# Zero products at the head and in four gaps of TensorE's program, token copies on VectorE, shared PSUM places for the leading tiles

## The chip, the core and the metric

The kernel runs on one core of one Trainium2 chip. The metric is the device time of one launch in microseconds (us), the median over several runs. PE is TensorE's matmul stream, PEld its weight loads, DVE is VectorE, ACT ScalarE, POOL GpSimdE and SP SyncE, which here only issues transfers.

## The reference

Two layers of a diffusion trunk run over 512 latent tokens and 128 context tokens of width 2048, all in float32. Cut to what matters here:

```python
for layer in range(DEPTH):                      # 2 layers: even, odd
    sh_p, sc_p, gt_p = modulation(c_ctx, ada_w[layer], ada_b[layer])   # silu(cond) @ w + b, three parts
    sh_s, sc_s, gt_s = modulation(c, ada_w[layer], ada_b[layer])
    hp = rms_norm(xp, norm_g[layer]) * (1.0 + sc_p) + sh_p
    hs = rms_norm(xs, norm_g[layer]) * (1.0 + sc_s) + sh_s
    # input projection h @ w_in, two mixers (attention / short conv or two attentions),
    # SiLU gates, output projection
    xp = xp + gt_p * out_p
    xs = xs + gt_s * out_s
```

So before the first large product (layer 0's h @ w_in) can start, the kernel needs the tokens with their features on the partitions, each token's norm factor, and the scale and shift parts of the modulation, which are themselves products of silu(cond) with 2048-row weights.

## The kernel before, in words

All products take a float32 weight and a float32 operand apart into a high and a low part and add three products (`proj_q`, `one_block`, `lead_units`). The split of a weight is an ACT copy (line 227) and a DVE subtraction (line 228).

The order on each engine is not the order of the source: a planner at build time puts the instructions of each engine into a fixed order, by their place in the source, by what they wait for and by its own times. `tc.issue_after(x)` pins what the block emits on the engine of `x` behind `x`. At run time each engine goes through its own order and waits where something isn't ready.

**The head.** `x_load` brings five blocks of 128 tokens, two halves each, on ACT's and SP's queues. The conditions `c` and `c_ctx` land in rows 0 to 31 of `rows_a`; a Tanh on ACT (`th`, line 122) and a DVE step (line 123) make SiLU of them, PE transposes them (line 126) and DVE writes `sT`, the operand of every modulation product. `first_loads` then gives the order of the head: `x_block` for each block of tokens, `vec_rows` (transposes of small vectors, line 131), `ada_on_pe` for the scale of the first 128 features, `x_rows` (the norm factors spread over all partitions, lines 975 and 976), and `ada_on_pe` for the shift.

`x_block` transposes a block in four groups of four 128x128 transposes (line 960), each group into a PSUM place of `psT` (two places, tag T, shared by every small use in the kernel), and copies each group to `xT` (line 961): groups 0 to 2 on DVE, group 3 on ACT. ACT squares each half of a block into a PSUM place (line 965) for the norm, DVE and POOL finish it (lines 967 to 969).

`ada_on_pe` loads 1 MB or more of modulation weights (line 169, four buffers), multiplies on PE (line 180, 32 instructions for 16 products: a full-precision product is two instructions), copies, transposes (line 186) and reduces.

**The leading tiles.** `lead_units` then runs eight column tiles of the input projection at once, two rows of features (k) at a time, while the modulation for the next features is still being made: `make_h(k)` is `h0_maker`, `ahead` is `ada_group`, the modulation of the features to come. Unit 0 takes k = 0 (`c = 0`) and k = 1 (`c = 1`) one after the other. Six of the tiles are summed in SBUF and pass through PSUM place 0 (`new_pp(0)`, halves pa and pb), two (`held`) stay in PSUM. The first products are on lines 359 to 361, those of later units on lines 263 to 265. Weight pieces of these tiles come through buffers of tag `raw` (four of them), which `rows_a`, `rows_b` and `th` also use before.

After that `run_tiles` goes on tile by tile. `new_pp` gives PSUM places in turn and writes each into the list `whole`; `bank_of` gives a job that has staged such a tile the tile's own PSUM place for its transposes, and otherwise a T place. Of the leading tiles this concerns the key tile (`k_gen`: staged by `stage`, line 626, transposed on line 633, read on lines 663 to 668).

## Time and profile before

| what | value |
|---|---|
| three runs | 2281.19, 2277.36, 2281.74 us (median 2281.19) |
| the profiled execution's own time | 2278.45 us |
| its span, first to last instruction | 2276.6 us |
| DVE, ACT, POOL busy | 1602.2, 1087.0, 162.7 us |
| granted clock | 1.0 in every window of the profile |
| moved | 337.64 MB, mean 148 GB/s |

A row of the timeline gives start and length in us, engine, line, operation, output and inputs, shape, count, and in brackets the engine's idle time before it and what ended it. A row of the groups gives count, busy us and mean ns, then idle us before and its causes. Ends of matmuls are modelled, and they are pipelined, so starts are to be read rather than ends.

### The profile page before, as it was taken

The page shows a single profiled execution, that of the slowest core. Times are in us where ns is not written, and L with a number is a line of the kernel's source. Part 1 is how long each engine was busy: PE and PEld are TensorE (multiplying, and loading weights), DVE is VectorE, ACT ScalarE, POOL GpSimd, SP SyncE. Part 2 cuts the span into 40 slices and gives each one's busy share as a digit, 9 for nine tenths or more (in the row PEclk, how much of TensorE's full clock was granted, in tenths as well). Part 3 has the DMA queues.
Part 4 walks back from the last instruction along what each step waited for, and adds up shares of the span by engine and source line. Part 5 has one row for each costly group of instructions (what it writes and reads, how often), then busy time and mean ns, then how long its engine had stood idle before and what let it go on. Part 6 is the DMA issues. An engine that isn't in the chain of part 4 may idle for free.

```text
span 2276.6 us, 41019 instructions
## 1 busy us (share of the span) xinstructions
PE 2245.3 (99%) x15941; PEld 2173.6 (95%) x15941; DVE 1602.2 (70%) x2830; ACT 1087.0 (48%) x2281; POOL 162.7 (7%) x226
## 2 busy tenths in 40 slices
PE   7999999999999999999999999999999999999999
PEld 5889999999999999999999999999999999999999
DVE  5666969779779777887797666565666655557865
ACT  5224535245352222544474444565565676754443
POOL 1001000010000000000100001111111100000101
PEclk9999999999999999999999999999999999999999
DMA  9975545655647565745553333423223221238542
GB/s 323 321 224 174 178 148 165 184 162 169 182 122 231 174 189 158 231 146 148 163 167 105 115 111 113 146 70 100 86 61 101 69 64 57 71 105 256 150 134 62
DMA packets 382514, 337.64 MB, mean 148 GB/s; under 512 B 16098, under 2 KB 342208, under 8 KB 381808
## 3 DMA queue, kind: packets, MB, share of 16 engines
q1 hardware_dynamic: 367744, 290.10, 42.7%
q0 software_dynamic: 13856, 42.76, 5.5%
q8 instruction: 125, 2.05, 0.4%
q10 hardware_dynamic: 720, 2.16, 0.3%
q14 instruction: 69, 0.57, 0.1%
HBM read 295.37 MB, written 39.59 MB: 147 GB/s over the span
## 4 chain that ended last, share of the span: by engine, by line
PE 90%; DMA 4%; DVE 2%; ACT 2%; issue 2%; SPq 0%; POOL 0%; POOLq 0%; ACTq 0%; DVEq 0%
PE pq L606 7%; PE pq L605 7%; PE pq L604 7%; PE pa L263 6%; PE pa L264 6%; PE pb L264 6%; PE pb L263 6%; PE pb L265 6%; PE pa L265 6%; PE pa L277 3%; PE pb L278 3%; PE pb L279 3%; PE pb L277 3%; PE pa L279 3%; PE pa L278 3%; PE T L808 2%
## 5 line engine op out<-in xcount | busy, mean ns | idle before, releaser
L227 ACT ACTIVATE wh<-raw 128x512 fp32r<-128x512 f32 x418 | 263.7, 631 | 545.0 <-PE pb L264 384.9
L228 DVE TENSOR_TENSOR wl<-raw,wh 128x512 fp32r<-128x512 f32 x418 | 288.0, 690 | 199.9 <-ACT wh L227 191.9
L263 PE MATMUL pa<-h,wh 128*128 128x320 f32 x978 | 310.1, 318 | 3.4 <-ACT h L227 1.7
L264 PE MATMUL pa<-h,wh 128*128 128x320 f32 x978 | 304.3, 312 | 2.0 <-DVE h L228 1.8
L265 PE MATMUL pa<-h,wl 128*128 128x320 f32 x978 | 302.9, 310 | 0.0
L264 PE MATMUL pb<-h,wh 128*128 128x320 f32 x978 | 302.5, 309 | 0.0
L265 PE MATMUL pb<-h,wl 128*128 128x320 f32 x978 | 302.4, 309 | 0.0
L263 PE MATMUL pb<-h,wh 128*128 128x320 f32 x978 | 301.6, 309 | 0.7 <-ACT h L1435 0.7
L205 DVE SCALAR_TENSOR_TENSOR acc<-adaw,sT,acc 128x1024 f32<-128x1024 f32 x240 | 300.6, 1280 | 0.2 <-DMA adaw<-in_ada_w 0.2
L604 PE MATMUL pq<-h,wh 128*128 128x320 f32 x672 | 208.6, 310 | 0.0
L606 PE MATMUL pq<-h,wl 128*128 128x320 f32 x672 | 207.7, 309 | 0.0
L605 PE MATMUL pq<-h,wh 128*128 128x320 f32 x672 | 207.7, 309 | 0.0
L263 PEld LDWEIGHTS pa<-h,wh 128*128 128x128 f32 x978 | 183.6, 188 | 16.6 <-issue 9.1
L264 PEld LDWEIGHTS pa<-h,wh 128*128 128x128 f32 x978 | 184.0, 188 | 7.8 <-issue 4.1
L263 PEld LDWEIGHTS pb<-h,wh 128*128 128x128 f32 x978 | 183.3, 188 | 1.4 <-ACT h L1435 0.9
L264 PEld LDWEIGHTS pb<-h,wh 128*128 128x128 f32 x978 | 183.6, 188 | 0.9 <-issue 0.8
L265 PEld LDWEIGHTS pa<-h,wl 128*128 128x128 f32 x978 | 183.7, 188 | 0.4 <-issue 0.4
L265 PEld LDWEIGHTS pb<-h,wl 128*128 128x128 f32 x978 | 183.6, 188 | 0.0
L605 PE MATMUL pq<-T,wh 128*128 128x320 f32 x504 | 155.2, 308 | 0.0
L606 PE MATMUL pq<-T,wl 128*128 128x320 f32 x504 | 155.1, 308 | 0.0
L604 PE MATMUL pq<-T,wh 128*128 128x320 f32 x504 | 155.0, 308 | 0.0
L277 PE MATMUL pa<-h,wh 128*128 128x320 f32 x448 | 146.5, 327 | 0.0
(488 smaller groups left out, 5410.8 us busy)
## 6 DMA issues: line engine op xcount, KB each, us to landing
adaw<-in_ada_w SPq DMA_DIRECT2D x128, 512.0 KB, 4.2
raw<-in_ev_w_in SPq DMA_DIRECT2D x176, 256.0 KB, 3.4
raw<-in_od_w_in SPq DMA_DIRECT2D x154, 256.0 KB, 2.9
ada<-in_ada_w SPq DMA_DIRECT2D x32, 1024.0 KB, 9.7
w<-in_od_w_in SPq DMA_DIRECT2D x27, 512.0 KB, 3.9
yd<-y POOLq DMA_DIRECT2D x32, 320.0 KB, 3.3
w<-in_ev_w_out SPq DMA_DIRECT2D x18, 512.0 KB, 4.7
w<-in_od_w_out SPq DMA_DIRECT2D x18, 512.0 KB, 4.3
```

Of the source, the lines that this page charges most:

```text
L205: V.scalar_tensor_tensor(out=acc[c], in0=w, scalar=sT[:, kt, c:c + 1], in1=acc[c], op0=ALU.mult, op1=ALU.add)
L227: A.activation(hi, x, AF.Copy)
L228: V.tensor_sub(lo, x, hi)
L263: PE.matmul(ps, wh[:, i, :], hi[:, sl], start=(j == js[0] if alone else (pos == 0 and j == 0)), stop=False)
L264: PE.matmul(ps, wh[:, i, :], lo[:, sl], start=False, stop=False)
L265: last_mm[j % 4] = PE.matmul(ps, wl[:, i, :], hi[:, sl], start=False, stop=(j == js[1] - 1 if alone else (pos == 3 and j == 3)))
L277: PE.matmul(ps, wh[:, j, :], hi[:, sl], start=(qd == 0 and j == 0), stop=False)
L278: PE.matmul(ps, wh[:, j, :], lo[:, sl], start=False, stop=False)
L279: PE.matmul(ps, wl[:, j, :], hi[:, sl], start=False, stop=(qd == 3 and j == 3))
L604: PE.matmul(ps, wh[:, j, :], hi, start=(new and h == 0 and j == 0), stop=False, **kw)
L605: PE.matmul(ps, wh[:, j, :], lo, start=False, stop=False, **kw)
L606: PE.matmul(ps, wl[:, j, :], hi, start=False, stop=(h == 1 and j == 3), **kw)
```

## The change

1. A tile `cold` of zeros is made on DVE; ACT takes a Tanh of one column of it ahead of all else.
2. `keep_warm(n)` multiplies `cold` with itself n times on PE into a PSUM tile that nobody reads: 14 times ahead of the first transpose, 8 times after block 0 and its vectors, 4 times within block 1, 6 times between the two calls of `x_rows`, 4 times behind the shift product.
3. `x_block` transposes into PSUM places pa0, pb0, pa1, pb1 of the projection in place of the two T places; all copies but one (block 3, group 3) go to DVE; the squares are written to SBUF (tag h5) in place of PSUM.
4. The scale product stands between blocks 3 and 4 in the source, before it stood behind block 4.
5. The modulation of feature block 1 (`ahead(0, (1, 2))`) stands at leading tile 3 in place of tile 1, its PE instructions pinned behind the last product so far.
6. `rows_a`, `rows_b` and `th` get tiles of their own in place of weight buffers.
7. Five small loads (gains, band, sink) are pinned behind the last modulation load on SP.
8. `new_pp` writes only the later tiles into `whole`, so the jobs of leading tiles transpose into T places.
9. The first weight splits of the leading tiles are pinned on ACT behind the last square of block 4 in place of its last copy.

```diff
+    cold = pre.tile([P, P], F32, name="cold")
+    V.memset(cold, 0.0)
+    A.activation(cold[:, 0:1], cold[:, 0:1], AF.Tanh)
+    rows_a = pre.tile([P, P], F32, name="rows_a")
...
+    warm = pS.tile([P, 1024], F32, tag="S", name="warm")
+    def keep_warm(n):
+        for _ in range(n):
+            PE.matmul(warm[:, 0:P], cold, cold, start=True, stop=True)
+    keep_warm(14)
...
-    def new_pp(i):
+    def new_pp(i, own=False):
...
-        whole.extend(pp)
+        if own:
+            whole.extend(pp)
...
-                    if i == 1 and ui == 0 and c == 0:
-                        ahead(0, (1, 2))
-                    elif i == 1 and ui + 1 < len(units):
+                    if i == 3 and ui == 0 and c == 0:
+                        with tc.issue_after(last_mm[0].ins):
+                            ahead(0, (1, 2))
+                    elif i == 1 and (ui or c) and ui + 1 < len(units):
                         ahead(*units[ui + 1][1:])
...
-            pp = new_pp((i - lead) % 2)
+            pp = new_pp((i - lead) % 2, True)
...
+    sqj = hpool.tile([P, 1024], F32, tag="h5", name="sqj")
     def x_block(b, ts):
-            ta = psT()
+            ta = pproj.tile([P, 512], F32, tag="p" + ("a0", "b0", "a1", "b1")[g], name="ta")
...
-            put[0] = (A.copy if g == 3 else V.tensor_copy)(xT[g][:, :, b * P:(b + 1) * P],
+            (A.copy if g == 3 and b == 3 else V.tensor_copy)(xT[g][:, :, b * P:(b + 1) * P],
...
+            if b == 1 and g == 1:
+                keep_warm(4)
             if g % 2 == 0:
-                junk = pS.tile([P, 1024], F32, tag="S", name="sqj")
-                A.activation(junk, ts[g // 2], AF.Square, accum_out=s4[:, g // 2:g // 2 + 1])
+                put[0] = A.activation(sqj, ts[g // 2], AF.Square, accum_out=s4[:, g // 2:g // 2 + 1])
...
         x_block(0, xs[0])
         vec_rows(0, 80, rows_a, 32)
-        for b in range(1, 5):
+        keep_warm(8)
+        for b in range(1, 4):
             x_block(b, xs[b])
+        ada_on_pe(0, 4, 0, 1, scale)
+        x_block(4, xs[4])
         last_act[0] = put[0]
-        ada_on_pe(0, 4, 0, 1, scale)
         x_rows((0, 1, 2, 3))
+        keep_warm(6)
         x_rows((4,))
         vec_rows(80, 77, rows_b, 0)
         ada_on_pe(0, 0, 0, 1, shift)
+        keep_warm(4)
```

More of the change, by code (lines that the diff above doesn't have):

```diff
@@ L94, in trunk_kernel @@
     sp = pre = pools["cur"]
-    rows_a = wpool.tile([P, P], F32, tag="raw", name="rows_a")
+    cold = pre.tile([P, P], F32, name="cold")
+    V.memset(cold, 0.0)
+    A.activation(cold[:, 0:1], cold[:, 0:1], AF.Tanh)
+    rows_a = pre.tile([P, P], F32, name="rows_a")
     def x_load(b):
@@ L109, in trunk_kernel @@
     xs = [x_load(b) for b in range(5)]
-    rows_b = wpool.tile([P, P], F32, tag="raw", name="rows_b")
+    rows_b = pre.tile([P, P], F32, name="rows_b")
     nc.gpsimd.dma_start(rows_b[0:48, :], I["ada_b"][1].rearrange("(k p) -> k p", p=P))
@@ L115, in trunk_kernel @@
         nc.gpsimd.dma_start(rows_b[74 + i:75 + i, :], I[n])
+    last_ada = [None]
     ada_t = [pre.tile([P, 2048], F32, name=f"ada{i}") for i in range(4)]
@@ L119, in trunk_kernel @@
     h_t = [pre.tile([P, NT], F32, name=f"ht{i}") for i in range(2)]
-    th = wpool.tile([32, P], F32, tag="raw", name="th")
+    warm = pS.tile([P, 1024], F32, tag="S", name="warm")
[3 more added lines that the diff above has]
+    keep_warm(14)
+    th = pre.tile([32, P], F32, name="th")
     A.activation(th, rows_a[0:32, :], AF.Tanh, scale=0.5)
@@ L168, in ada_load @@
         ada_t.append(ada_t.pop(0))
-        nc.sync.dma_start(w, I["ada_w"][l, kt * P:(kt + m) * P, cb * 512 + b0 * P:cb * 512 + (b0 + n) * P]
+        last_ada[0] = nc.sync.dma_start(w, I["ada_w"][l, kt * P:(kt + m) * P, cb * 512 + b0 * P:cb * 512 + (b0 + n) * P]
                           .rearrange("(k p) n -> p k n", p=P))
@@ L960, in x_block @@
                 PE.transpose(ta[:, j * P:(j + 1) * P], ts[g // 2][:, o:o + P], ident)
-            put[0] = (A.copy if g == 3 else V.tensor_copy)(xT[g][:, :, b * P:(b + 1) * P],
-                                                           ta.rearrange("p (j t) -> p j t", j=4))
+            (A.copy if g == 3 and b == 3 else V.tensor_copy)(xT[g][:, :, b * P:(b + 1) * P],
+                                                             ta.rearrange("p (j t) -> p j t", j=4))
+            if b == 1 and g == 1:
+                keep_warm(4)
             if g % 2 == 0:
-                junk = pS.tile([P, 1024], F32, tag="S", name="sqj")
-                A.activation(junk, ts[g // 2], AF.Square, accum_out=s4[:, g // 2:g // 2 + 1])
+                put[0] = A.activation(sqj, ts[g // 2], AF.Square, accum_out=s4[:, g // 2:g // 2 + 1])
         ss = small.tile([P, 1], F32, tag="nm", name="ssx")
@@ L981, in ada_group @@
         if g == 3 and js[1] == 4:
-            for i, n in enumerate(("a_k_norm", "c_k_norm", "d_k_norm")):
-                load_rows(gain_rows[:, i, :], n)
-            nc.sync.dma_start(band, I["k_band"])
-            load_rows(sink, "a_sink")
+            with tc.issue_after(last_ada[0].ins):
+                for i, n in enumerate(("a_k_norm", "c_k_norm", "d_k_norm")):
+                    load_rows(gain_rows[:, i, :], n)
+                nc.sync.dma_start(band, I["k_band"])
+                load_rows(sink, "a_sink")
     def first_loads(cols):
```

## The prediction

> **What bounds the kernel now.** I read the page first, then the table by windows, then the timeline of the first 36 us, then the waits and the neighbourhood of the first key tile.
>
> ```profile
> span 2276.6 us, 41019 instructions
> PE 2245.3 (99%) x15941; PEld 2173.6 (95%) x15941; DVE 1602.2 (70%) x2830; ACT 1087.0 (48%) x2281; POOL 162.7 (7%) x226
> ```
>
> TensorE (PE) is busy for 99% of the span. So a change in the head is worth what it takes off the moment from which PE no longer stops; nothing behind that moment shortens by it.
>
> ```profile
> 0.00:10.00 10.00, 1.34 (x6) 1.28 (x7) 1.06 (x5) 3.27 (x5) 4.37 (x12) 1.00 0.80 267
> 20.00:30.00 10.00, 7.76 (x104) 5.58 (x102) 6.35 (x15) 4.73 (x11) 0.55 (x1) 1.00 1.15 315
> 30.00:40.00 10.00, 8.24 (x101) 6.78 (x102) 6.00 (x16) 6.18 (x15) 0.00 (x0) 1.00 1.12 336
> 40.00:50.00 10.00, 10.00 (x99) 6.45 (x98) 3.36 (x9) 3.57 (x9) 0.00 (x0) 1.00 1.00 307
> 150.00:160.00 10.00, 10.00 (x105) 7.66 (x105) 5.89 (x16) 1.38 (x3) 0.00 (x0) 1.00 0.43 116
> ```
>
> Columns: the window, its length, busy us (and count) of PE, PEld, DVE, ACT, POOL, then granted clock, DMA share, GB/s. PE idles for 8.7, 2.2 and 1.8 us in the first three rows and not in the fourth. The transfers are full (share 1.00 to 1.15, 307 to 336 GB/s) from 20 to 50 us and half idle (0.43) by 150 us: in the head, loads are a second bound right behind PE.
>
> ```profile
> 6.68 1.28 ACT L122 ACT_TABLE_LOAD   x1 [6.68 <-DMA rows_a<-in_c_ctx]
> 8.65 0.31 PE L126 MATMUL T<-ident,rows_a 32*128 32x32 f32 x1 [8.65 <-DVE rows_a L123]
> 8.89 3.87 PE L960 MATMUL T<-ident,xb 128*128 128x128 f32 x16
> 12.36 1.03 ACT L965 ACTIVATE sqj<-xb 128x1024 f32<-128x1024 f32 x1 [0.67 <-DMA xb<-in_x_sample]
> 19.11 1.14 PE L960 MATMUL T<-ident,xb 128*128 128x128 f32 x8 [0.19 <-DVE xT L961]
> 21.99 1.14 PE L960 MATMUL T<-ident,xb 128*128 128x128 f32 x8 [0.19 <-DVE xT L961]
> 24.77 0.59 ACT L961 COPY xT<-T 128x512 f32<-128x512 f32 x1 [2.35 <-PE T L960]
> ```
>
> PE's first work waits until 8.65 for a Tanh whose table load starts only when its rows have landed. The first 16 token transposes take 3.87 us (0.24 each); later 8 take 1.14 (0.14). Blocks of 16 then repeat every 2.88 us (19.11 to 21.99), with PE waiting for copies out of two PSUM places; the last copy ends at 25.36.
>
> ```profile
> 26.50 1.29 PE L975 MATMUL T<-ident,rx 128*128 128x128 f32 x10
> 28.45 1.08 PE L180 MATMUL T<-ada,sT 128*32 128x128 f32 x32
> 31.16 1.08 PE L180 MATMUL T<-ada,sT 128*32 128x128 f32 x32 [0.86 <-DMA ada<-in_ada_w]
> 32.18 0.56 PE L359 MATMUL pa<-h,wh 128*128 128x320 f32 x2
> 34.63 1.08 PE L180 MATMUL T<-ada,sT 128*32 128x128 f32 x32 [0.90 <-DMA ada<-in_ada_w]
> 35.64 0.42 PE L360 MATMUL pa<-h,wh 128*128 128x320 f32 x1
> ```
>
> The leading tiles start at 32.18; the shift product that they need starts at 28.45, 3.73 us earlier. Two modulation loads then hold PE for 0.86 and 0.90 us. From 35.64 on PE no longer stops for the head.
>
> **The change, part by part.** *Early table load.* A Tanh on a memset tile takes the load (1.28) off the wait for rows_a: the first transpose moves from 8.65 to about 7.4. On the other side, standing ahead of the input loads that ACT issues, it could hold them by the same 1.28, and the head with them; it waits for a memset while they wait for nothing, so I take the gain.
>
> *14 zero products at the head.* L975 shows the form: five full-precision products are ten instructions in 1.29 us, 0.26 per product. They run from about 2 us, when only loads are under way. At the slow rate of the first 16 transposes (0.24 per instruction) 28 instructions take 6.7 us, at the later one 3.9: they end between 6 and 8.7, against 7.4 for the first real transpose, so they cost between 0 and 1.3. I take 0.3. What they bring: block 0's transposes drop from 3.87 to some 2.2.
>
> *22 zero products in four gaps* (8, 4, 6, 4): 22 x 0.26 = 5.7 us of PE. Twelve stand among transposes, where PE needs 4 x 16 x 0.14 = 9.0 of the 4 x 2.88 = 11.5 us of four blocks and also waits for block 1 (the ACT row at 12.36 shows its second half landing at 12.3); that covers their 3.1 us. The six (1.6) and the last four (1.0) stand around the norm rows and the shift product, in the stops between 27.8 and 32.2. Without that cover they put up to 2.6 us on the chain. As clock keepers I price them at nothing: the transposes at 19.11 already run at the fast rate with nothing but transposes ahead of them. [...]
>
> *Copies.*
>
> ```profile
> L227 ACT ACTIVATE wh<-raw 128x512 fp32r<-128x512 f32 x418 | 263.7, 631 | 545.0 <-PE pb L264 384.9
> ...
> L965 ACT ACTIVATE sqj<-xb 128x1024 f32<-128x1024 f32 x10 | 10.3, 1027 | 0.8 <-DMA xb<-in_x_sample 0.7
> L961 DVE COPY xT<-T 128x512 f32<-128x512 f32 x15 | 10.1, 690 | 3.2 <-PE T L960 2.9
> L961 ACT COPY xT<-T 128x512 f32<-128x512 f32 x5 | 2.9, 582 | 2.4 <-PE T L960 2.3
> L967 DVE TENSOR_REDUCE ssx<-s 128x1 f32<-128x2 f32 x5 | 0.8, 153 | 0.3 <-ACT sqj L965 0.2
> ```
>
> Four of ACT's five copies go to DVE: 4 x 0.69 = 2.76 and two small operations of 0.15 make at most 3.06 us of DVE a block, somewhat less where copies overlap in part. That is the old pace of 2.88, not a faster one. The gain is that four PSUM places (pa, pb) replace two, so PE and ACT no longer wait in turn. With block 0 copied by 10.8, block 1 bound by its landing (12.3, done by 14.3) and three blocks at 2.9, the last copy ends at about 22.9 instead of 25.36. The squares now write SBUF; 1.03 us, or by two of the 512-wide writes to SBUF (631 ns) at most 1.3, twice a block, stays under DVE's 3.
>
> *Scale product ahead of the last block.*
>
> ```profile
> L169 SPq DMA_DIRECT2D ada<-in_ada_w x1: 520/520/520, 10.9 to 10.9; - x1
> DMA to landing us min/median/max: 10.2/10.2/10.2
> ...
> L169 SPq DMA_DIRECT2D ada<-in_ada_w x1: 467/467/467, 18.1 to 18.1; - x1
> DMA to landing us min/median/max: 7.2/7.2/7.2
> ...
> L169 SPq DMA_DIRECT2D ada<-in_ada_w x1: 2532/2532/2532, 35.8 to 35.8; - x1
> DMA to landing us min/median/max: 11.8/11.8/11.8
> 47.30 1.93 PE L180 MATMUL T<-ada,sT 128*32 128x256 f32 x32
> ```
>
> The scale load lands at 10.9 + 10.2 = 21.1, the shift load at 18.1 + 7.2 = 25.3. If PE meets the scale product ahead of block 4, block 4's transposes, copies, norm and rows queue behind a stop until 21.1: 1.08 + 4 x 0.69 + 0.6 brings the last copy to about 25.5, and no gain is left in that chain but its overlap. If block 4 goes first, the shift load is the bound: 25.3 + 3.73 = 29.0 for the leading tiles, against 32.18. I take 29.2, **3.0 us earlier**; the other order gives about 30.7, 1.5 earlier.
>
> *Modulation of block 1 behind lead tile 2.* It moves two loads' products behind three leading tiles (18 products) and so behind their landings (31.1 and 34.6); the 0.86 and 0.90 us of stops go, but 1.08 us of product that lay ahead of 32.18 now lies behind: even, 0.
>
> *rows_a, rows_b, th out of the weight buffers.*
>
> ```profile
> SPq L336 <- DVE mod L163: 4.0, 1, 4.0
> ```
>
> SP stood 4.0 us at a weight load until a buffer came free. That stop goes; since the transfers are full, little lands earlier (0 to 0.8 us). The five small loads pinned behind the last modulation load keep their place: 0.
>
> *Leading key tile frees its own PSUM.*
>
> ```profile
> 198.53 0.60 PE L633 MATMUL pa<-ident,stg 128*128 128x128 f32 x4
> 201.60 0.69 DVE L665 TENSOR_TENSOR kg<-pa,gain_rows 128x512 f32<-128x512 f32 x1
> 202.35 0.42 PE L263 MATMUL pa<-h,wh 128*128 128x320 f32 x1 [1.71 <-DVE kg L665]
> ```
>
> The key tile transposes into pa, and the next tile's products wait 1.71 us until kg has been read. With a shared T place pa is free as soon as it is staged: **1.7 us** go, at best. At worst PE meets the next transpose, which needs a T place too, with both held until 202.3, and the stop stays: 0.
>
> Sum on the profiled execution: 2278.45 (span 2276.6) - 3.0 - 1.7 = 2273.75. The median of the runs, 2281.19, lies 2.74 above that execution; the same 4.7 off gives 2276.5, or 0.21%.
>
> **Rivals.** *Capped by the loads.* PE's order is fixed beforehand. The fourth load of the next unit lands at 35.8 + 11.8 = 47.6; its second half of products in the block at 47.30 starts near 48. That leaves about 0.4 us. If the block keeps its place in the order while all moves up by 3.0, PE stops there for the rest and the head yields only 0.4 to 1.3. For it: the full share from 20 to 50 us. Against: behind 47.30 there are still unit-0 products that the order can draw ahead, and SP's 4.0 us stop goes. With the key tile: 1.5 to 3.0 off, 2278.2 to 2279.7.
>
> *The change doesn't do what it says.* The zero products wait for nothing, so the plan may put all 36 at the front: 72 instructions, 28 slow (6.7) and 44 at 0.13 (5.7), until about 14 us, past block 0's data. The head then ends where it did, with the key tile's 0 to 1.7: about 2280.5.
>
> *Slower: scores ahead of their softmax.*
>
> ```profile
> PE S L820 <- ACT p L794: 2.1, 4, 1.5
> ```
>
> The order behind the head is planned anew. Today score products wait for the softmax that still holds S four times, 1.5 us at the longest. If the new order puts the two attention stages a step earlier, each such place costs 1.5; the even layer has 40 score steps (4 pairs of heads, 5 blocks, 2 heads). It decides from four such stops, which eat the 4.7; at seven it is 10.5 - 4.7 = 5.8 slower, 2287. For it: a gap that closes early moves every filler. Against: only one long stop today, with the same plan rules.
>
> **How the numbers follow.** What a measurement of this kernel can tell from no change is about 0.2%, 4.6 us. The forecast case (head 2.5 to 4, key tile 1 to 1.7) has 0.46, capped 0.29, no effect 0.08, slower 0.17. Of the forecast case nearly all but 0.06 lies beyond 0.2%, and 0.02 of the capped one with luck elsewhere: faster 0.42; same 0.06 + 0.27 + 0.08 = 0.41; slower 0.17. The range: the forecast case with its upper bounds (head 4.1, that is the shift load's 3.2 and one of the two stops; key tile 1.7; two of the 1.5 us stops gone by luck) is 8.8 off, 2272; at the other end no effect and the mild slower outcomes, +3, 2284; beyond lies some 0.2.
>
> **What would show it.** Right: the first transpose near 7.4 and 16 of them in about 2.2 us; last xT copy near 23; L359 near 29; no DMA stop over 1 us at L180 from 38 to 50; no wait of L263 on kg. Capped: L180 waiting on ada for 1.5 to 3 us near 45. All products in front: L960 starting past 10. Slower: L820 waits above 8 us in total. I am wrong in kind if L359 starts later than 31.5, or if PE's waits behind 210 us change by more than the head does.

## The result, and the profile after

The changed kernel takes 2284.71 us (median of 7 runs, 2283.12 to 2287.5) against 2277.36 (7 runs, 2275.66 to 2281.95): ratio 1.0029, 95% interval 1.0019 to 1.0038. (The 2281.19 that I forecast from was the median of the first three of the seven runs before.) The change costs some 6.6 us (the interval says 4.3 to 8.7), where I had forecast 4.7 us less. The profiled execution, page first, then the table by windows (window, length, busy us of PE, PEld, DVE, ACT, POOL, then granted clock, DMA share, GB/s):

```profile
span 2283.2 us, 41163 instructions
...
PE 2258.0 (99%) x16013; PEld 2185.8 (96%) x16013; DVE 1602.1 (70%) x2835; ACT 1083.9 (47%) x2278; POOL 162.2 (7%) x226
```

```profile
0.00:10.00 10.00, 7.26 (x43) 7.26 (x44) 1.63 (x6) 3.54 (x6) 4.36 (x12) 1.00 0.77 254
20.00:30.00 10.00, 7.58 (x62) 6.39 (x63) 3.86 (x11) 4.21 (x9) 1.10 (x2) 0.66 1.05 298
30.00:40.00 10.00, 7.99 (x93) 6.77 (x96) 5.42 (x15) 4.63 (x11) 0.99 (x1) 1.00 1.13 323
40.00:50.00 10.00, 9.88 (x115) 6.83 (x107) 3.62 (x10) 5.05 (x14) 0.00 (x0) 1.00 0.92 283
```

The span is 6.6 us longer and PE is busy 12.7 us longer, with 72 instructions more (the 36 zero products). The new thing stands in the second row: from 20 to 30 us the granted clock is 0.66, and PE gets through 62 instructions where it did 104. (The 1.00 of the first row is no measurement up to 8.01 us: the first full clock is on record there, before at 12.65.) All seven runs of the changed kernel have a mean granted clock of 0.997 or 0.998, while 22 of the 27 runs of before measured beside b_ahead have 0.999 or 1.000, so the profiled execution is no exception. The timeline of PE in the head shows why:

```profile
2.74 5.89 PE L129 MATMUL warm<-cold 128*128 128x128 f32 x28 [2.74 <-ACT cold L97]
8.47 1.91 PE L975 MATMUL ta<-ident,xb 128*128 128x128 f32 x16
...
22.41 0.64 PE L192 MATMUL T<-ada,sT 128*32 128x128 f32 x2 [3.09 <-DMA ada<-in_ada_w]
22.98 1.97 PE L975 MATMUL ta<-ident,xb 128*128 128x128 f32 x8
24.88 1.93 PE L192 MATMUL T<-ada,sT 128*32 128x128 f32 x30
26.74 1.76 PE L975 MATMUL ta<-ident,xb 128*128 128x128 f32 x7
...
30.38 1.95 PE L129 MATMUL warm<-cold 128*128 128x128 f32 x16
32.69 0.49 PE L991 MATMUL T<-ident,rx 128*128 128x128 f32 x2 [0.36 <-POOL rx L985]
...
33.53 1.08 PE L192 MATMUL T<-ada,sT 128*32 128x128 f32 x32
...
36.59 0.56 PE L372 MATMUL pa<-h,wh 128*128 128x320 f32 x2 [1.21 <-ACT h L1034]
```

PE's program has one product of the scale block (two instructions) ahead of the last 8 transposes of block 3. It stops there for 3.09 us until the load lands at 22.4, with transposes queued behind it whose data are there by 16.9 (the last token load of blocks 0 to 3 is issued at 5.3, and none takes over 11.6 to land). The eight that follow take 1.97 us; before, eight took 1.14. The windows around it:

```profile
18.00:21.60 3.60, 1.32 (x11) 1.08 (x10) 3.06 (x7) 3.50 (x7) 0.55 (x1) 1.00 0.96 260
21.70:28.40 6.70, 5.99 (x48) 4.79 (x49) 1.26 (x3) 2.24 (x7) 0.00 (x0) 0.50 1.11 313
28.60:36.00 7.40, 5.98 (x72) 5.15 (x70) 4.45 (x15) 1.40 (x5) 1.53 (x2) 1.00 1.14 307
```

The clock is 0.50 from 21.7 to 28.4. By its records the stretch lasts 6.83 us, twice the 3.41 of the shortest drops below. PE was not idle all through before it: in the 3.41 us that end where the clock falls it was busy for 1.08 (last section). At the rows above the half clock costs 0.83 (8 transposes), 0.9 (30 of the scale instructions, 1.93 against 32 in 1.08) and 0.8 (7 transposes, 1.76 against some 1.0): 2.5 us.

So the first leading product starts at 36.59, **4.41 us later** than 32.18. To follow the difference on, I set PE's instructions, zero products left out, side by side in their order: the start of the n-th in one kernel less that of the n-th in the other. The changed kernel is 5.5 us behind at 45 us, 8.0 at 190, and 5.6 from 350 to 915 us. The 2.4 given back at about 205 us are the key tile: from 196 to 212 us PE has no wait any more, on kg or anything else. The 2.5 lost between 45 and 190 us are not stops. Modulation products now stand in smaller groups between leading tiles (before first, then after):

```profile
55.72 1.05 PE L180 MATMUL T<-ada,sT 128*32 128x256 f32 x10
...
60.87 1.07 PE L180 MATMUL T<-ada,sT 128*32 128x256 f32 x16
...
77.81 1.93 PE L180 MATMUL T<-ada,sT 128*32 128x256 f32 x32
```

```profile
81.42 0.62 PE L192 MATMUL T<-ada,sT 128*32 128x256 f32 x2
84.80 1.93 PE L192 MATMUL T<-ada,sT 128*32 128x256 f32 x30
```

Here "x2" and "x30" are instructions of one block of 32. A group of two takes 0.62 us, and 30 take as long as 32. By starts (ends are modelled), from the last product ahead of a group to the first behind it, it is 0.79 us for 2, 1.24 for 16 and 2.10 for 30 or 32. With the 0.147 that lies between two leading products anyway, dividing a block into 2 and 30 costs 0.64 and into 16 and 16 costs 0.23. From the start to the first key tile PE's program switches between modulation and other work 52 times before and 62 after. From 45 to 190 us the same 422 modulation instructions stand in 18 groups before and in 22 after (two blocks divided into 2 and 30, two into 16 and 16), and the times of these groups add up to 1.8 us more, out of the 2.5. Where the rest lies was not separated.

### The profile page after: what moved, and what is told of

Read it like the earlier page. It is cut to its first block, busy times and chain, and to the rows that moved or that the text cites. A ratio compares the mean times of both kernels' runs of the same rounds, so it can differ in the third digit from the quotient of the medians.

```text
span 2283.2 us, 41163 instructions
## 1 busy us (share of the span) xinstructions
PE 2258.0 (99%) x16013; PEld 2185.8 (96%) x16013; DVE 1602.1 (70%) x2835; ACT 1083.9 (47%) x2278; POOL 162.2 (7%) x226
## 4 chain that ended last, share of the span: by engine, by line
PE 90%; DMA 3%; ACT 2%; DVE 2%; issue 2%; POOL 0%; SPq 0%; ACTq 0%; POOLq 0%; DVEq 0%
PE pq L620 7%; PE pq L619 7%; PE pq L618 7%; PE pa L275 6%; PE pa L276 6%; PE pb L275 6%; PE pa L277 6%; PE pb L276 6%; PE pb L277 6%; PE pa L289 3%; PE pb L290 3%; PE pb L291 3%; PE pb L289 3%; PE pa L291 3%; PE pa L290 3%; PE T L822 2%
## 5 line engine op out<-in xcount | busy, mean ns | idle before, releaser
L275 PEld LDWEIGHTS pa<-h,wh 128*128 128x128 f32 x978 | 183.7, 188 | 12.7 <-issue 7.8
```

The costliest lines, as they stand in the source:

```text
L275: PE.matmul(ps, wh[:, i, :], hi[:, sl], start=(j == js[0] if alone else (pos == 0 and j == 0)), stop=False)
```

## The experiments

My theory (W): the stop at the scale load and the half clock behind it make the loss; finer mixing of modulation and leading products (later G, "places") adds to it. The rivals: the zero products stand on the chain (F), the scale product's source place is what counts (P), and for each part, that it is worth what I had priced.

"Behind" is the difference just described, from one profiled execution of each; ratios are to the kernel before, measured beside it. "Half clock" is the time at clock 0.5 up to 45 us, counted from when the clock first was full, which differs by execution: 6.1 to 20.2 us, 12.65 before, 8.01 after.

| kernel | switches | first leading product | half clock, us | behind at 45 / 190 / 350 us | ratio (95%) |
|---|---|---|---|---|---|
| before | 52 | 32.18 | 0 | 0 | 1 |
| after | 62 | 36.59 | 6.83 | 5.5 / 8.0 / 5.6 | 1.0029 (1.0019, 1.0038) |
| scale_pinned | 60 | 29.92 | 0 | 1.0 / 3.3 / 0.8 | 1.0017 (1.0008, 1.0026) |
| stall_covered | 54 | 31.87 | 0 | 2.3 / 3.7 / 1.5 | 1.0001 (0.9993, 1.0010) |
| place_only | 66 | 34.41 | 3.41 | 3.3 / 5.7 / 3.2 | 1.0020 (1.0011, 1.0029) |
| key_only | 52 | 32.70 | 0 | -0.3 / 0.5 / -2.1 | 0.9989 (0.9980, 0.9997) |
| pin_nogap | 58 | 29.22 | 3.41 | 1.7 / 2.9 / 0.8 | 1.0001 (0.9991, 1.0010) |
| pin_nofill | 56 | 28.79 | 6.83 | 1.2 / 1.9 / -0.5 | 0.9995 (0.9986, 1.0004) |
| b_places | 64 | 33.44 | 13.65 | 6.5 / 8.3 / 8.7 | 1.0040 (1.0028, 1.0053) |
| key_head | 54 | 32.87 | 3.41 | 1.3 / 1.6 / -0.9 | 0.9993 (0.9985, 1.0002) |
| key_head2 | 52 | 32.08 | 3.41 | 0.3 / 0.2 / -2.4 | 0.9988 (0.9980, 0.9997) |
| after_no_places | 54 | 33.70 | 3.41 | 3.2 / 4.0 / 1.5 | 1.0010 (1.0001, 1.0019) |
| no_places_pinned | 54 | 33.09 | 6.83 | 2.7 / 3.6 / 1.1 | 1.0003 (0.9993, 1.0012) |
| no_places_ahead | 54 | 33.10 | 6.83 | 2.9 / 3.8 / 1.3 | 0.9991 (0.9982, 1.0000) |
| b_ahead | 56 | 31.75 | 0 | -0.3 / 1.8 / 1.2 | 1.0016 (1.0007, 1.0025) |
| b_table | 52 | 34.37 | 0 | 1.8 / 1.6 / 2.2 | 1.0001 (0.9992, 1.0009) |
| key_table | 52 | 32.41 | 3.41 | 0.0 / -0.1 / -2.5 | 0.9990 (0.9981, 0.9999) |
| after_ahead | 68 | 35.36 | 3.41 | 4.3 / 6.6 / 4.0 | 1.0034 (1.0021, 1.0047) |
| rest_ahead | 58 | 32.68 | 0 | 0.6 / 2.5 / 0.1 | 1.0001 (0.9992, 1.0010) |
| rest_behind | 58 | 34.03 | 6.83 | 1.4 / 3.2 / 0.7 | 0.9998 (0.9989, 1.0007) |

**The stop and the half clock.** In the first, the scale product goes behind block 4 and is tied to its last transpose:

```diff
...
-        ada_on_pe(0, 4, 0, 1, scale)
         x_block(4, xs[4])
         last_act[0] = put[0]
+        with tc.issue_after(last_tr[0].ins):
+            ada_on_pe(0, 4, 0, 1, scale)
```

> The changed kernel with the scale product moved back behind block 4 and its PE instructions pinned behind block 4's last transpose. Theory W (wait and clock): in the changed kernel one scale product stood ahead of block 4's transposes, PE waited 3.09 us for its load, and that stop halved the clock for 6.8 us. Without it: no window below 1.00 in the granted clock, no DMA wait above 0.5 us before the transposes end, first leading product (36.59 in the changed kernel) at 30 to 32, span 3.5 to 6.5 us below the changed kernel's 2283.2, so within 3 us of the kernel before. Rival F (fillers): the zero products in the gaps hold the chain; they are all still there, so the first leading product stays at 35 or later and the span within 1.5 us of 2283.2.

In stall_covered 13 zero products are tied behind block 3 and the scale product behind them, ahead of block 4:

```diff
...
-        ada_on_pe(0, 4, 0, 1, scale)
+        with tc.issue_after(last_tr[0].ins):
+            keep_warm(13)
+        with tc.issue_after(last_w[0].ins):
+            ada_on_pe(0, 4, 0, 1, scale)
         x_block(4, xs[4])
```

> The changed kernel with 13 more zero products (2.9 us at 0.224 each) pinned on PE between block 3's transposes and the scale product, which is pinned behind them; the wait for the scale load stays, but PE is busy in it. Theory W with both parts: the clock never falls, the load still sets the place of block 4; first leading product at 33 to 34 (some 2.5 to 3.5 earlier than 36.59), span 2.5 to 4 below 2283.2. If the wait alone matters and the slow clock was off the path: first leading product at 36 or later and the span within 1 us of 2283.2. Rival F (more zero products cost more): span above 2283.2.

In place_only the scale product's call goes behind block 4 in the source, with nothing tied:

> The changed kernel with the scale product moved back behind block 4 in the source, and nothing pinned. Theory W says that the place in the source is not the cause: with four places for the transposes the planner has T places free and puts scale products ahead of block 4 all the same (one of them in PE's order still stands ahead of 24 transposes), so a DMA wait of about 3 us at the scale product and a clock below 1.00 between 20 and 30 us stay, span 5 to 8 above the kernel before. Rival P (the source place is the cause): as with the pinned product, span within 3 us of the kernel before.

PE's timeline of place_only, then windows of scale_pinned and of stall_covered:

```profile
22.19 0.64 PE L192 MATMUL T<-ada,sT 128*32 128x128 f32 x2 [3.92 <-DMA ada<-in_ada_w]
```

```profile
20.00:30.00 10.00, 7.16 (x104) 5.86 (x102) 5.76 (x19) 4.71 (x12) 1.10 (x2) 1.00 1.04 292
...
1140.00:1145.00 5.00, 5.00 (x24) 5.00 (x25) 5.00 (x12) 3.39 (x8) 0.00 (x0) 0.66 0.36 103
2096.00:2101.00 5.00, 4.48 (x19) 4.22 (x20) 4.04 (x8) 1.16 (x2) 0.00 (x0) 0.66 0.97 292
```

```profile
20.00:30.00 10.00, 8.96 (x124) 8.10 (x123) 5.10 (x14) 2.91 (x7) 1.10 (x2) 1.00 1.03 282
```

Source place is not the cause: place_only still has one product planned ahead and stops for 3.92 us. Without the stop, or with the stop filled, the clock stays at 1.00 and the first leading product comes 4.7 to 6.7 us earlier than in the changed kernel. Theory W holds in direction; in stall_covered it undersold itself (31.87, forecast 33 to 34). That kernel does not price the clock alone: its pins also take block 3's last eight transposes out from behind the product and leave 54 switches. Of the forecast spans two were missed: place_only's is 2.9 us above before where W said 5 to 8, and scale_pinned's is 2283.5 where W said 3.5 to 6.5 below 2283.2.

scale_pinned is not faster than before although its first leading product is 2.26 earlier, because the load of the next modulation block now ends last. Its waits of PE from 18 to 60 us:

```profile
PE T L192 <- DMA ada<-in_ada_w: 2.4, 2, 2.1
PE T L198 <- ACT ada_sb L195: 1.3, 2, 0.8
PE pa L372 <- ACT h L1035: 1.2, 1, 1.2
```

That is what the prediction's rival "capped by the loads" forecast, with two differences: the stop is at 36.9 us, not near 45, and the load is not only met earlier, it also lands later. SP's timeline before, then in scale_pinned:

```profile
18.70 4.53 SPq L336 DMA_DIRECT2D raw<-in_ev_w_in  x4
23.28 3.39 SPq L169 DMA_DIRECT2D ada<-in_ada_w  x2
```

```profile
19.27 6.53 SPq L349 DMA_DIRECT2D raw<-in_ev_w_in  x6
25.84 7.05 SPq L181 DMA_DIRECT2D ada<-in_ada_w  x3
```

In the new order six weight loads stand ahead of the third and fourth modulation load in place of four, and the fourth lands at 36.8 where it landed at 34.5; PE reached its product at 34.8. All thirteen kernels with six there have the fourth landing between 35.1 and 38.0, the seven with four between 34.2 and 35.4. The weight buffers that the change sets free allow this order, but b_places has it without them, so it is not tied to one part.

The windows at 1140 and 2096 us show two further clock drops of 3.41 us in this execution, which others of the same kernels lack or have elsewhere; they make single executions differ by some us at the end, which is why "behind" is read up to 350 us. They also bear on the ratio: six of scale_pinned's twelve runs have a mean granted clock of 0.999 and take 2278.3 to 2281.5 us, the six with 0.996 to 0.998 take 2282.2 to 2287.3.

**The key tile alone** (the argument own of new_pp, and nothing else, in the kernel before):

```diff
-    def new_pp(i):
+    def new_pp(i, own=False):
...
-        whole.extend(pp)
+        if own:
+            whole.extend(pp)
...
-            pp = new_pp((i - lead) % 2)
+            pp = new_pp((i - lead) % 2, True)
```

> The kernel before with one part of the change alone: only later tiles are entered in the list, so the leading key tile transposes into T places. If the key tile's part is right: the 1.71 us wait of L263 on kg (202.35 in the kernel before) is gone and the span is 1.5 to 2.5 below 2276.6. If later stops take it back or T places are short: a new wait of PE between 198 and 212 us, span within 0.5 of 2276.6 or above.

2.1 us by the trace at 350 us, 0.9989 by the runs: as forecast. The span of the profiled execution, 2279.1, is not below 2276.6 as the forecast had it; its clock was half for 10.2 us between 2065 and 2097.

**The four places, and the gap products.** pin_nogap is scale_pinned without the 22 gap products, pin_nofill without the 14 at the head as well. b_places is the kernel before with one line changed, `ta = psT()` into the four places of pproj.

> The pinned kernel (scale product behind block 4) without the 22 zero products in the four gaps; the 14 at the head stay. Theory W (the wait for the scale load and the half clock behind it made the loss; the gap products lie in idle time): first leading product 29 to 30.5 as in the pinned kernel (29.92), the PE stop of 2.1 us for the next modulation load stays, time within 1.5 us of the pinned kernel's 1.0017 of before, so 1.0010 to 1.0024. Rival F (the gap products stand on the chain, 16 instructions each of 0.12 to 0.13 at two places): first leading product 26.5 to 28.5 and the time 2 to 3 us lower, 1.0003 to 1.0009. Theory C (without them the clock falls in the gaps): granted clock below 1 before 40 us, leads later than 31.

> The pinned kernel (scale product behind block 4, four places) without any zero product; against the same without the 22 gap products alone (leads at 29.22, 1.0001 of before) it tells what the 14 at the head are worth. Theory B (the head products only bring the full clock forward; the head is bound by landings and copies): first transpose 6.8 to 7.6 in place of 8.06, 16 transposes in 3.5 to 3.9, first leading product 28.7 to 30, time 0.9994 to 1.0006. Rival K (they matter: without them the clock is still half when the later blocks run): full clock only after 17 us, first leading product 30.5 or later, time 1.0007 to 1.0020.

> The kernel before with one part of the change: the token transposes of a block go through four PSUM places of the leading tiles (pa, pb) in place of two shared T places; who copies is as before. Theory G (the places decide the order that is planned: products of modulation and of leading tiles are mixed more finely, at 0.2 to 0.3 us a switch): no early scale product, last copy 23 to 24.5 in place of 25.4, first leading product 30.5 to 32 in place of 32.18, but PE behind the kernel before by 1 to 3 us from 110 to 195 us relative to that lead, and the time 0 to 2 us above before (1.0000 to 1.0010). Rival H (places are a gain and the mixing comes from the block-1 modulation moved behind tile 2): lead kept to 195 us, time 0.5 to 1.5 us below before (0.9993 to 0.9998).

PE's timeline of b_places, and a window of it:

```profile
28.29 0.80 PE L975 MATMUL T<-ident,rx 128*128 128x128 f32 x2 [2.80 <-POOL rx L969]
```

```profile
27.30:40.90 13.60, 10.79 (x83) 7.45 (x84) 3.60 (x11) 3.71 (x9) 0.55 (x1) 0.50 1.09 313
```

The places by themselves are the dearest part, 1.0040. PE runs through the transposes sooner, then stops 2.80 us for the last norm row, and the clock is half for 13.65 us behind that stop: the same sequence as behind the scale load's stop, at another wait. I had forecast 0 to 2 us for it, so theory G had the mixing (64 switches, 1.8 us from 45 to 190) and missed the clock; neither theory's time held. The gap products cost 0.7 us of the first leading product (29.92 to 29.22); the ratios (1.0017, and 1.0001 where theory W said 1.0010 to 1.0024) lie further apart than that explains, and I leave the rest open. Without them the clock did fall, for 3.41 us from 14.0, among the transposes, and that cost nothing that the time shows. In pin_nofill, without a zero product, full clock came at 7.9 with nothing but transposes ahead, and the time is no worse: the 36 products are worth nothing in that kernel.

**The head's parts.** key_head is the key tile with the change's head (Tanh ahead of the loads, 14 products). In key_head2 the Tanh stands behind the scalar engine's loads and writes a tile of its own, with 12 products; key_table is that with none. (In key_head and key_head2 the products write a T place.) b_table is the kernel before with the memset and the early Tanh alone.

> The kernel before with two parts of the change: the key tile's own PSUM place, and the head (early Tanh on the memset tile, 14 zero products that wait for it). Theory W (the head products hold the first transpose as long as the table load did, and the loads on the scalar queue come later): first transpose 8.3 to 8.7, 16 transposes in 1.9 to 2.2, last copy 24.5 to 25.5, first leading product 31.5 to 32.5, so time as with the key tile alone (0.9989): 0.9985 to 0.9993. Rival N (the head's faster clock carries through): first leading product 30 to 31.4 and 0.9980 to 0.9985. Rival L (the table load ahead of the loads costs its 1.28): first leading product 33 or later, 0.9993 to 1.0000.

> The same two parts, but the Tanh stands behind the scalar engine's input loads and writes a tile of its own, so that no load stands behind the table load and the 12 zero products wait for the memset alone. Theory W: zero products start below 2 and end by 6.5 to 7, first transpose 7.2 to 7.6, scale load lands at 21 to 21.3 as before, first leading product 30.5 to 32.2, time 0.9978 to 0.9989 of before. Rival P (PE's pace from block 1 on is set by copies and landings, whatever the head does): first leading product 31.9 to 32.4 and time 0.9986 to 0.9992, as with the key tile alone.

> The kernel before with one part alone: a memset and a Tanh ahead of the input loads. Theory L (the table load stands on the scalar engine ahead of three of its four token loads): those land 0.8 to 2.5 us later than 6.22, 9.58 and 12.28, block 1's transposes wait for them, first leading product 0 to 1.5 us later, time 1.0000 to 1.0008. Rival G (as priced: the first transpose 1.2 us earlier carries through): first transpose 7.3 to 7.6, first leading product 31 to 31.9, time 0.9990 to 0.9998.

> The kernel before with the key tile's own place and the early Tanh behind the scalar engine's input loads, without any zero product: a candidate for the best version. First transpose 7.2 to 7.6, loads land as before. Theory P (copies and landings set the pace from block 1 on): first leading product 31.7 to 32.3 and 0.9985 to 0.9991, level with the key tile alone (0.9989) and with the 12 zero products added (0.9988). Rival H (head products were worth something in that kernel): 0.9991 to 0.9998 here.

The scalar engine's timeline of b_table, then PE's:

```profile
0.75 0.42 ACTq L104 DMA_DIRECT2D xb<-in_x_sample  x1
1.20 1.28 ACT L97 ACT_TABLE_LOAD   x1 [1.20 <-PEq L1817]
1.62 0.85 ACTq L104 DMA_DIRECT2D xb<-in_x_sample  x2
```

```profile
7.15 0.31 PE L129 MATMUL T<-ident,rows_a 32*128 32x32 f32 x1 [7.15 <-DVE rows_a L126]
...
15.88 10.16 PE L963 MATMUL T<-ident,xb 128*128 128x128 f32 x52 [2.79 <-ACT xT L964]
...
34.37 0.56 PE L362 MATMUL pa<-h,wh 128*128 128x320 f32 x2 [0.20 <-ACT h L1016]
```

The first transpose is 1.5 us earlier and the first leading product 2.2 later: two of the four token loads are issued 0.4 us later behind the Tanh, the last of the four lands at 14.1 in place of 12.3, and the copies fall behind. Over all kernels that last landing is at 12.6 to 14.7 us in the twelve with the Tanh ahead of the loads and at 12.0 to 12.3 in the other eight; the scale load lands at 21.1 to 22.6 and at 20.8 to 21.2. So theory L holds for the landings. Its bound of 1.5 us is not refuted, because a second thing differs in this execution: its clock was full only from 20.2 us on, and the 52 transposes from 15.88, which run across that moment, take 10.16 us, 0.20 each, between the 0.24 of the first 16 (3.87) and the 0.16 of the eight at 26.29 (1.25). In key_only, whose head is that of before, a first full clock at 17.6 came with a first leading product 0.5 later. The runs do not tell b_table from before (1.0001). The early Tanh behind the loads does no harm (key_table), and none of these heads is worth anything beside the key tile: key_head 0.9993, key_head2 0.9988, key_table 0.9990, key_only 0.9989.

**Block 1's modulation behind leading tile 2.** b_ahead does that part alone; after_ahead undoes it in the changed kernel:

> The kernel before with one part alone: the modulation of block 1 moves behind leading tile 2. Theory A (the third modulation product used to fill the wait for the first h): first leading product 31 to 31.5 in place of 32.18, but a stop of 1.2 us ahead of it and the 1.08 us product behind it, PE 0.3 to 1.0 us behind the kernel before from 60 us on; where the granted clock falls for 3.4 us behind that stop, another 1.5: time 1.0002 to 1.0012. Rival E (even, as priced): within 0.3 us at 60 us and 0.9997 to 1.0003. Rival W (two loads' stops of 0.86 and 0.90 go): 1 to 1.8 us ahead at 60 us, 0.9990 to 0.9996.

> The changed kernel with one part undone: the modulation of block 1 stands ahead of leading tile 1 again. The planned order then switches 68 times between modulation and other products in place of 62, and the scale product still stands among block 3 and 4's transposes. Theory A (the move costs by itself): no stop of 1.2 us for h ahead of the first leading product. Theory G (with the four places the order gets finer still): the stop at the scale load stays (2 to 4 us) with half the clock behind it, PE 6 to 9 us behind before from 110 to 195 us, time 1.0025 to 1.0045, no better than the change. Rival: it is better by 0.5 us or more, 1.0012 to 1.0025.

PE's waits of b_ahead from 18 to 60 us, and its modulation products around 55 us (before: 10, 6 and 16 at a time, from 55.72 to 61.9):

```profile
PE pa L359 <- ACT h L1014: 1.2, 1, 1.2
...
PE T L180 <- DMA ada<-in_ada_w: 0.4, 1, 0.4
```

```profile
54.33 1.02 PE L180 MATMUL T<-ada,sT 128*32 128x256 f32 x10 [0.43 <-DMA ada<-in_ada_w]
56.35 0.63 PE L180 MATMUL T<-ada,sT 128*32 128x256 f32 x6
58.28 0.62 PE L180 MATMUL T<-ada,sT 128*32 128x256 f32 x2
59.46 0.64 PE L180 MATMUL T<-ada,sT 128*32 128x256 f32 x8
61.98 0.63 PE L180 MATMUL T<-ada,sT 128*32 128x256 f32 x6
```

The stop for h is there as theory A says, 1.2 us that the third modulation product had filled. It is even at 45 us, as I had priced it, and then loses 2.1 by 190 us through smaller groups of products (the 16 at 60.87 before are 2, 8 and 6 here); 1.0016, more than any of the theories gave. That after_ahead is no better (1.0034, 68 switches, stop 3.66 us at the scale load) fits: the parts act through one planned order and do not add.

**Without the four places.**

> The changed kernel with one part undone: the token transposes go through the two shared T places again; zero products, copies, key tile and the source place of the scale product are the change's. In the planned order modulation and leading products now switch 54 times in place of 62 (52 before), and the scale product stands whole ahead of block 4. Theory G (the four places bring the mixing, worth about 3 us of the loss by 110 us, and let PE reach the scale product early): PE reaches the scale product with under 1.5 us of stop, the granted clock stays 1.0 between 18 and 40 us, first leading product 31.5 to 33.5, PE behind the kernel before grows by less than 0.7 us from 45 to 195 us, time 0.9985 to 1.0003 of before. Rival W (the scale product ahead of block 4 is enough): stop of 2 us or more, a half-clock stretch of 3.4 us or more, leads at 34 or later, 1.0008 to 1.0025.

> The changed kernel with three parts undone: the four places (two shared T places again), the 22 gap products, and the scale product's place (pinned behind block 4's last transpose). Head products, copies by the vector engine, key tile and the block-1 modulation behind tile 2 stay. Theory G: first leading product 31 to 32.5, no stop at the scale load over 0.3 us, growth from 45 to 195 us under 0.7, key tile gives back 2; time 0.9980 to 0.9993. Rival M (moving block 1's modulation behind tile 2 costs by itself): growth of 1.5 to 3 us, 0.9995 to 1.0005.

> As the pinned one, but with the scale product in source order ahead of block 4 and not pinned: it differs from that one by the scale product's place alone. Theory W (a product met before its load lands stops PE, and a stop near 3 us is followed by half the clock): if PE reaches the product 1.5 us or more before the load (landing at about 22), the stop shows in full, and with 2.5 us or more the clock falls to 0.5 for 3.4 us; leads 1.5 to 5 us later than the pinned kernel and the time 0.0006 to 0.0020 above it. Rival T (with two T places the transposes come late enough): stop below 0.5 us, leads within 0.5 us and the time within 0.0005 of the pinned one.

With two T places again and all else as changed, PE no longer stops at the scale load, the switches fall from 62 to 54 and the time from 1.0029 to 1.0010 (theory G had forecast 0.9985 to 1.0003, and full clock throughout). That one undone part takes back about two thirds of the loss (the two intervals just touch). Half clock stays (3.41 to 6.83 us in these profiles); in all three one drop begins between 33.4 and 34.7 us, at or behind the 1.2 us stop for h. A window of no_places_pinned:

```profile
33.50:36.80 3.30, 3.30 (x15) 3.27 (x14) 1.65 (x4) 1.73 (x4) 0.00 (x0) 0.50 1.05 306
```

15 products there; at the full clock's 0.147 us it would be 22: 1.1 us lost in 3.3. no_places_pinned came between its theories (0.9 us lost from 45 to 190 us, and a time in M's range). no_places_ahead came out 0.0012 below it, with intervals that overlap: T was right on the first leading product (33.10 against 33.09), not on the stop (0.88 us, forecast below 0.5), and W's price does not show at such a stop.

**What is left of the head.** The changed kernel without the four places, without zero products, with the Tanh behind the loads and block 1's modulation in its old place; the scale product ahead of block 4, or behind it:

> The changed kernel without its four places, without any zero product, with the early Tanh behind the scalar engine's loads and block 1's modulation ahead of leading tile 1 again. Left of the change: key tile, copies by the vector engine, squares into SBUF, small tiles out of the weight buffers, scale product ahead of block 4. Theory P (landings and copies set the head): scale load lands at 21 to 21.3, stop at it below 0.5 us, first leading product 31.3 to 32.4, time 0.9983 to 0.9992 of before, no better than the key tile alone (0.9989) by more than 0.0005. Rival B (without its costs the head's rest is a gain): first leading product below 31, 0.9970 to 0.9983.

> The same with the scale product behind block 4 in the source. Theory P: within 0.0005 of the kernel with it ahead; first leading product 31.8 to 32.5. Rival B: 31 or below and below 0.9983. Rival C (the copies by the vector engine slow the blocks): first leading product above 32.6, 0.9990 to 1.0000.

Both are level with before, so theory P's 0.9983 to 0.9992 for the first was missed. rest_behind came out as rival C said (34.03, 0.9998), but its clock was half for 6.83 us of the head, so slower copies by the vector engine are not shown. Both keep the key tile's 2.4 and lose 1.8 between 45 and 190 us at 58 switches. Which of the parts left makes the order finer was not separated. The best versions are the key tile alone, key_head2 and key_table: some 2.5 us, 0.1%, below before.

## Why the prediction was wrong

*Early table load.* Wrong in sign. I saw that the Tanh could hold the scalar engine's input loads and took the gain; alone it brings the first transpose to 7.15 and, in the one execution profiled, the first leading product 2.2 us back, part of it by a late full clock. In the changed kernel the last of its four loads lands at 14.7, before at 12.3.

*14 zero products at the head.* Mis-sized: they end at 8.5, since they wait for the Tanh at 2.74 (I had them start at 2), and hold the first transposes there, not at 7.4. The 16 transposes do drop to 1.91. It carries through to nothing, as block 1 waits for its load.

*22 zero products in four gaps.* About right: 0.7 us where I took 0, within the 2.6 I had named. As clock keepers in front of transposes they were rightly priced at nothing (pin_nofill, 0.9995). None stood where the clock fell: the stop ahead of the scale product had no filler in PE's order.

*Copies.* Right where nothing stops PE: the last copy ends at 22.9 in scale_pinned, as forecast. In the changed kernel it ends at 30.8, behind the stop.

*rows_a, rows_b, th out of the weight buffers.* Nothing lands earlier. SP's 4.0 us stop is gone, but the third and fourth modulation load land at 32.2 and 35.8, before at 31.0 and 34.5; SP issues two weight loads more ahead of them, an order that b_places has without this part.

*Scale product ahead of the last block.* **This is the step that failed.** I took block 4 first, 29.2, and gave 30.7 for PE meeting the product first. PE met it first, even ahead of half of block 3, and the cost was 36.59. The step lacked three terms: the load lands at 22.4, not 21.1, since the loads ahead of it slid behind the Tanh; the stop is followed by 6.83 us of half clock (2.5 us by the rows); and the four places make the planner put the product there at all. I had read granted clock 1.00 in every row of the head of before as a fact of the chip, not of an order that had no stop over 1 us there. Mending this step alone would not have saved the forecast: scale_pinned, without the stop, has its first leading product at 29.9, near my 29.2, and the key tile's gain, and is still 0.8 us behind before at 350 us. There the later modulation load (2.1 us) and the finer order (2.3 us) take the gain back.

*Modulation of block 1.* Right for the first 45 us, wrong as a whole: 1.2 us of stop opened and, by 190 us, 1.8 were lost.

*Order behind the head.* I had a rival for a finer order, but put it at the scores. The waits there did not grow (S on p: 1.8 us, four times, before 2.1). It came at the modulation products, 2.5 us, which I priced at nothing.

*Key tile.* Right: 1.7 forecast, 2.1 to 2.6 given back at about 205 us in the kernels that have it.

By my own signs I was wrong in kind: the first leading product started later than 31.5.

## What to carry to other kernels

An instruction moved ahead in an engine's fixed order is priced by what is queued behind it when its data are late (here block 3's last eight transposes, behind a stop of 3.09 us), and on PE by the half clock that followed such stops here (6.83 us behind 3.09, 13.65 behind 2.80), not by the stop alone. In these profiles the cases are ordered by how much of a 3.41 us window the stops took together: where the clock fell, PE had been busy for 0.67 of one at most (last section). Buffers given to an early stage change the order that a planner writes for the next: count the switches between kinds of product in the new order, and how they divide the blocks, before counting gains. Filling a gap with zero products helped only where the stop was (13 there, with their pins, brought the first leading product from 36.59 to 31.87; the 22 in the gaps of scale_pinned put it 0.7 us later), and a bound behind it, here the modulation loads with 2.1 us, took back the rest.

## What was not expected of the hardware

- Behind a stop of 3.09 us (after) the granted clock was 0.50 for 6.83 us, behind one of 3.92 (place_only) for 3.41, behind one of 2.80 (b_places) for 13.65, though PE was busy for 10.8 of the 13.6 us in that window. The stop of 1.21 us for h was followed by a drop of 3.41 us in no_places_pinned (the row at 33.5) and by none in b_ahead or scale_pinned; every drop that ended within the span lasted 3.41 us or a multiple of it.
- Drops of the same length come late in some executions (near 1141 and 2066 to 2097 us) and not in others. They follow windows (see below) in which PE is busy for 0.41 to 0.67 of the time. The windows are laid out from the first full clock, which lies differently in each execution (12.65 before, 17.57 in key_only with the same head), so that the same stops can fall into one window or be shared by two; that this decides it was not tested.
- A group of two modulation products between leading tiles takes as long as one of eight (0.62 and 0.64 us); groups of 10 and 16 both take 1.05 to 1.07, and 30 and 32 both 1.93. Eight instructions are the four products that `kt % 4` sends to the four places of 32 partitions in T; whether the equal times come from that was not tested.

The length of 3.41 us is that of the clock's own records. In after the clock is full from 8.01 us, 0.50 from 21.66, full from 28.49 and 0.50 again from 2281.29: 4, 2 and 660 times 3.413 us apart. Before it is full from 12.65 to 2275.69, 663 times; in scale_pinned 332 times lie between the first full clock at 7.89 and the fall at 1141.11. It is not the length of the stop that orders these cases, but PE's busy share of the window of 3.41 us ahead, laid out from the first full clock of each execution. Windows of after (the clock falls behind the first, stays half behind the second, is full behind the third), then of place_only (falls, then full):

```profile
18.25:21.66 3.41, 1.08 (x10) 0.84 (x8) 2.81 (x7) 3.31 (x7) 0.55 (x1) 1.00 0.95 255
21.66:25.07 3.41, 2.65 (x14) 1.94 (x18) 0.75 (x2) 0.24 (x3) 0.00 (x0) 0.50 1.08 301
25.07:28.48 3.41, 3.41 (x38) 2.93 (x33) 0.58 (x1) 2.12 (x5) 0.00 (x0) 0.50 1.13 324
```

```profile
18.39:21.80 3.41, 0.00 (x0) 0.00 (x0) 1.62 (x5) 2.31 (x5) 0.55 (x1) 1.00 0.93 251
21.80:25.21 3.41, 3.02 (x18) 1.96 (x18) 0.75 (x2) 0.45 (x1) 0.00 (x0) 0.50 1.09 307
```

In before and after, 1327 such windows at full clock, it fell behind the three with PE busy for 0.15, 0.25 and 0.32, and behind no other, of which the lowest has 0.50. Over the twenty profiles I counted 13213. Behind all 10 with PE busy for less than 0.45 the clock fell, behind none of the 13140 with 0.68 or more, and behind 15 of the 63 between. At half clock (the time ahead of the first full clock included) it came back behind none of the 30 windows below 0.82 (0.78 at 21.66 in after), and behind 45 of the 50 from there on (1.00 at 25.07). These are counts of these profiles, with modelled busy times, and no limits of the chip; what decides between 0.45 and 0.68 stays open.
